# A hybrid attention decoder block on one core: compressed softmax without its table of valid blocks, and the gelu's reciprocals in quarters

## The chip, the cores and the metric

The kernel runs on one core of a Trainium2 chip. The metric is the device time of one execution in microseconds, as the median of several runs. Five engines of the core matter here and are named as the profile names them: PE (TensorE, matrix products and transposes; PEld is its weight load), DVE (VectorE), ACT (ScalarE), POOL (GpSimd) and SP, whose queue issues the DMAs.

## What is computed

Two layers, each a mixer and a gated feed-forward block, over 512 positions of width 1024. The mixer has three groups of heads beside each other: four "forgetting" heads (f), eight heads of native sparse attention (n) in three branches, and four dilated heads (d). The change touches the compressed branch of the n heads. There, keys and values are averaged into 31 blocks by a small network with a gelu, each query attends to the blocks that end at or before it, and the result is weighted by a gate:

```python
k_cmp = nsa_compress(kc, ...)            # gelu(win @ w1) @ w2
s_c = einsum('bqgrd,bngd->bgrqn', qb, k_cmp) * ATTN_SCALE
p_c = masked_softmax(s_c, cmp_end[None, :] <= qpos[:, None])
#   s = where(mask, scores, -1e30);  e = where(mask, exp(s - max), 0)
#   p = e / max(sum(e), 1e-30)
o_c = einsum('bgrqn,bngd->bqgrd', p_c, v_cmp)
o = gate_c * o_c + gate_s * o_s + gate_w * o_w       # gate = sigmoid(...)
```

The first 31 queries have no valid block, and their o_c is zero.

## The kernel before

All matrix products are made in three passes (high part by high part, high by low, low by high), and PE is the engine that most of the program is laid out around. Per layer there is the mixer's stage (here from about 60 to 310 us, and again from 737 to 987 us), in which a loop over units (lines 1240 to 1253) runs. A **unit** is one head, one branch and one of four tiles of 128 queries (t = 0 to 3). A **slot** is one pass of that loop. In a slot i the stages of several units are issued: the scores of unit i (`st_scores`), the maximum of unit i-1 on DVE (`st_max`, line 1126) and its exponential on ACT (`st_exp`, line 1131), the normalisation of unit i-2 (`st_norm`: a small reciprocal on DVE, line 1139, and a multiplication on POOL, line 1143), the transposes of unit i-4 on PE (`st_turn`, line 1156), their evacuation one slot later (lines 1167 and 1172), and the product with the values at i-7. Tiles t = 0 and t = 1 share one bank of scores, one reciprocal and one set of transposes. Unit 0 of layer 0 has its scores at 62 us; unit 33, the one named most below, has t = 1.

Between the stages a slot gives room to other work. First a **step** (`step`, line 1062) takes the next piece of the projections (`proj256`: dv, dq, dk and so on, four row tiles by two halves of the depth, in two PSUM banks), with a budget of 0.8 steps to a slot, so that every fifth slot (36, 41, 46, 51, 56) has none. Then `chain_step` (line 1069) moves the generator `cmp_pieces` (line 938) on by one `yield`: one piece of the compressed branch to a slot. At the slot's end, when the compressed probabilities are complete (`store["pc"]`) and a pair of heads has its sum, `cmp_values` (line 1212) issues the compressed branch's product with the values for one pair.

`cmp_pieces` goes through: the polynomial of the gelu on POOL (941 to 943), the split of w2 and the exponential (946 to 948), one addition and two reciprocals of half the columns each (950 to 952), the multiplication on POOL (954), an empty slot, two transposes (959), their evacuation (965 to 970), an empty slot, then 18 products into two PSUM tiles `pk` and `pv` (973 to 985), their evacuation to `kcm` and `vcm` (991 to 997). From there ten slots run a small softmax for the four query tiles, in which a tile's scores, exponential, normalisation, transposes and evacuation are issued at lags of 0, 1, 3, 5 and 6 slots (`c_scores`, `c_exp`, `c_norm`, `c_turn`, `c_keep`). In this trace the products `pk` and `pv` are issued in slot 40, the four `c_scores` in slots 42 to 45, the four `c_turn` in slots 47 to 50, and `cmp_values` for the first pair in slot 51, for the second in slot 55.

PSUM has eight banks in four tags: three of "acc", one of "o", two of "s", two of "pt". Projections hold two of "acc" at a time, and `cmp_pieces` takes its tiles from the same tag (CT = "acc"). `st_turn`, the transposes of the projections (line 737) and `cmp_values` take "pt". Rows of the softmax, rotated projections and the temporaries of `cmp_pieces` share ten SBUF buffers of the tag "r" (NROW).

Within this loop PE's order is the order of the program (`manual_schedule` for PE). The orders of DVE, ACT and POOL are not: a planner of the framework, with its own idea of durations, puts each instruction into its engine's queue, and the engine then takes them strictly in that order.

Of the kernel before, what the change touches and what calls it, by code (L numbers as in the profile page):

```python
# [9 lines left out]
F32 = mybir.dt.float32  # L10
# [3 lines left out]
ALU = mybir.AluOpType  # L14
# [10 lines left out]
NST = 4  # L25
# [49 lines left out]
def tile_hybrid_block(  # L75
# [6 lines left out]
    nc = tc.nc  # L82
    PS = bass.MemoryType.PSUM
    const = ctx.enter_context(tc.tile_pool(name="const", bufs=1))
# [10 lines left out]
    def nm(p):  # L95
        uid[0] += 1
        return f"{p}_{uid[0]}"
# [7 lines left out]
    def rt(shape=(128, 512), dt=F32):  # L105
        return rowp.tile(list(shape), dt, tag="r", name=nm("r"))

    def st(n, tag="sm"):
        return small.tile([128, n], F32, tag=tag, name=nm("sm"))
# [7 lines left out]
    def bc(ap, axis, n):  # L117
        a = ap.unsqueeze(axis)
        shape = list(a.shape)
        shape[axis] = n  # L120
        return a.to_broadcast(shape)
# [326 lines left out]
    for l in range(DEPTH):  # L448
# [129 lines left out]
        gates = small.tile([128, NST, 24], F32, tag="gates", bufs=1, name=nm("gates"))  # L578
# [35 lines left out]
        if l == 0:  # L614

            dint = rt(dt=I32)
            nc.gpsimd.iota(dint, pattern=[[-1, 512]], base=384, channel_multiplier=1)
            dflt = rt()
            nc.vector.tensor_copy(dflt, dint)
            cmask = const.tile([128, 512], F32, name="cmask")  # L620
            nc.vector.tensor_scalar(cmask, dflt, 0.0, BIG, op0=ALU.is_lt, op1=ALU.mult)
            dmask = const.tile([128, 512], F32, name="dmask")
            cnt = rt()
            nc.vector.tensor_scalar(cnt, dflt, 128.0, None, op0=ALU.is_le)
            for m in (3, 15):
                mi = rt(dt=I32)
                nc.vector.tensor_scalar(mi, dint, m, None, op0=ALU.bitwise_and)
                mf = rt()
                nc.vector.tensor_copy(mf, mi)
                nc.vector.scalar_tensor_tensor(cnt, mf, 0.0, cnt, op0=ALU.is_equal, op1=ALU.add)  # L630
            ge0 = rt()
            nc.vector.tensor_scalar(ge0, dflt, 0.0, None, op0=ALU.is_ge)
            nc.vector.tensor_mul(cnt, cnt, ge0)
            nc.vector.tensor_scalar(dmask, cnt, 0.0, BIG, op0=ALU.is_equal, op1=ALU.mult)
            for v, lg in ((2.0, -math.log(2.0)), (3.0, -math.log(3.0))):
                t = rt()
                nc.vector.tensor_scalar(t, cnt, v, lg, op0=ALU.is_equal, op1=ALU.mult)
                nc.vector.tensor_add(dmask, dmask, t)

            ci = rt((128, NST, 32))  # L640
            nc.gpsimd.iota(ci, pattern=[[128, NST], [-16, 32]], base=-31, channel_multiplier=1,
                           allow_small_or_imprecise_dtypes=True)
            cvalid = const.tile([128, NST, 32], F32, name="cvalid")
            nc.vector.tensor_scalar(cvalid, ci, 0.0, None, op0=ALU.is_ge)
            cinv = const.tile([128, NST, 32], F32, name="cinv")
            nc.vector.tensor_scalar(cinv, ci, 0.0, BIG, op0=ALU.is_lt, op1=ALU.mult)

            odd = const.tile([128, 2], F32, name="odd")
            oi = small.tile([128, 1], I32, tag="oi", bufs=1, name="oi")
            nc.gpsimd.iota(oi, pattern=[[0, 1]], base=0, channel_multiplier=1)  # L650
            nc.vector.tensor_scalar(oi, oi, 32, None, op0=ALU.bitwise_and)
            nc.vector.tensor_copy(odd[:, 1:2], oi)
            nc.vector.tensor_scalar(odd[:, 0:1], odd[:, 1:2], 0.0, None, op0=ALU.is_equal)
            nc.vector.tensor_scalar(odd[:, 1:2], odd[:, 1:2], 0.0, None, op0=ALU.is_gt)
            vcm = const.tile([128, 2, 2, 2, 64], F32R, name="vcm")

        nc.vector.tensor_scalar(gates, gates, 1.0, None, op0=ALU.add)
        nc.vector.reciprocal(gates, gates)

        mix, sums = {}, {}  # L660
        OFIRST = (0, 1, 2, 3)
# [88 lines left out]
        def main_pieces():  # L750
# [54 lines left out]
            def hidden(kv):  # L805
                while len(wins.get(kv, ())) < 2:
                    yield
                ph = ps("acc")
                for c in range(4):
                    hi, lo = getw(l, "w1", kv, c, pre=PRE)  # L810
                    for i in range(4):
                        j = 4 * c + i
                        w = wins[kv][j // 8][:, j % 8].rearrange("p u n -> p (u n)")
                        mm(ph[:, 0:256], w, hi[:, i, :], j == 0, False)
                        mm(ph[:, 0:256], w, lo[:, i, :], False, j == 15)
                    yield
                tmp = rt((128, 256))
                rows = slice(64 * kv, 64 * kv + 64)
                nc.scalar.activation(tmp[rows, :], ph[64:128, 0:256], AF.Copy)
                nc.vector.tensor_add(xc[rows, :], ph[0:64, 0:256], tmp[rows, :])  # L820
                if kv == 1:
                    chain.append(cmp_pieces(xc, w2r))
# [115 lines left out]
        def cmp_pieces(xc, w2r):  # L938

            t1, t2 = rt((128, 256)), rt((128, 256))  # L940
# [7 lines left out]
            nc.scalar.activation(t2, t1, AF.Exp, scale=-2.0 * math.sqrt(2.0 / math.pi))  # L948
            yield
            nc.vector.tensor_scalar(t2, t2, 1.0, None, op0=ALU.add)  # L950
            for c in range(2):
                nc.vector.reciprocal(t2[:, 128 * c:128 * c + 128], t2[:, 128 * c:128 * c + 128])
            yield
            nc.gpsimd.tensor_mul(xc, xc, t2)
            yield
            yield
# [38 lines left out]
            for u in range(2):  # L995
                nc.scalar.activation(vcm[:, :, 0, u, :], src, AF.Copy, scale=odd[:, u:u + 1])
                nc.vector.scalar_tensor_tensor(vcm[:, :, 1, u, :], src, odd[:, u:u + 1], f(vcm[:, :, 0, u, :]),
                                               op0=ALU.mult, op1=ALU.subtract)
# [26 lines left out]
            def c_norm(t):  # L1025
                row = rows[t]
                dn = st(8, "cm")
                nc.gpsimd.tensor_mul(row, row, bc(cvalid[:, t], 1, 8))
                nc.vector.tensor_reduce(dn, row, axis=AX.X, op=ALU.add)
                nc.vector.tensor_scalar(dn, dn, 1e-30, None, op0=ALU.max)  # L1030
                nc.vector.reciprocal(dn, dn)
                nc.vector.tensor_mul(dn, dn, gates[:, t, 0:24:3])
                nc.gpsimd.tensor_mul(row, row, bc(dn, 2, 32))
# [17 lines left out]
            for i in range(NST + CL[3]):  # L1051
                for lag, fn in zip(reversed(CL), (c_keep, c_turn, c_norm, c_exp)):
                    if 0 <= i - lag < NST:
                        fn(i - lag)
                if i < NST:
                    c_scores(i)
                yield
# [365 lines left out]
```

## Time and profile before

| | us |
|---|---|
| median of 3 runs | 1368.08 (1367.97 to 1368.92) |
| profiled execution, its own time | 1369.85 |
| its span, first to last instruction | 1367.9 |
| PE busy | 1338.0 |
| DVE busy | 850.4 |
| ACT busy | 728.2 |
| POOL busy | 287.0 |

The span is what the profiler saw between the first and the last instruction; the profiled execution's own time has 1.95 us around it. An engine is busy while one of its instructions runs; an idle time in brackets behind a row is the time that its engine stood still before it, with the instruction that is taken to have ended the wait. The name is inferred: of several awaited things it is the one that came last by the profile.

### The profile page before, as it was taken

What the parts mean: (1) busy time and instruction counts of PE and PEld (TensorE: products, weight loads), DVE (VectorE), ACT (ScalarE), POOL (GpSimd) and SP (SyncE); (2) the same over time, 40 slices, a digit from 0 to 9 for tenths busy, and PEclk for the clock granted to TensorE, in tenths of its full rate; (3) what the DMA queues carried; (4) which work ended last, traced back from release to release, by engine and by line L of the source; (5) the groups of instructions that cost most, each with busy time, mean ns of one, the idle gap of its engine ahead of it and who ended that gap; (6) DMA issues with size and microseconds to landing.
All of it is one profiled execution on the core that took longest, in us unless ns stands there. A gap on an engine that the chain in (4) does not pass through costs nothing.

```text
span 1367.9 us, 21028 instructions
## 1 busy us (share of the span) xinstructions
PE 1338.0 (98%) x7855; PEld 1177.9 (86%) x7855; DVE 850.4 (62%) x1893; ACT 728.2 (53%) x1506; POOL 287.0 (21%) x343
## 2 busy tenths in 40 slices
PE   9999999999999999999999999999999999999997
PEld 8899998978888888888898999999798888888886
DVE  7677787677755555433464887777876555554334
ACT  6567767777533333333465677667774333333232
POOL 2364753341000000000004647634210000000000
PEclk9999999999999999999999999999999999999999
DMA  6323311131333333333333242111323333332231
GB/s 181 94 63 115 104 35 48 58 128 33 107 93 103 97 92 96 104 93 123 111 96 93 63 139 63 47 41 58 120 62 98 103 92 93 104 97 92 94 122 62
DMA packets 145517, 123.74 MB, mean 90 GB/s; under 512 B 8264, under 2 KB 135688, under 8 KB 145416
## 3 DMA queue, kind: packets, MB, share of 16 engines
q1 hardware_dynamic: 145416, 122.40, 29.5%
q8 instruction: 62, 1.02, 0.3%
q14 instruction: 39, 0.32, 0.1%
HBM read 118.19 MB, written 4.19 MB: 89 GB/s over the span
## 4 chain that ended last, share of the span: by engine, by line
PE 85%; DVE 7%; ACT 4%; POOL 2%; issue 2%; DMA 0%; SPq 0%; ACTq 0%; POOLq 0%; DVEq 0%
PE acc L115 39%; PE s L115 19%; PE pt L115 13%; PE o L115 10%; PE pt L1156 3%; POOL wt L795 1%; PE pt L737 1%; DVE hl L271 1%; DVE pl L1172 1%; DVE r L1126 1%; ACT r L1131 1%; DVE x L913 0%; ACT hh L270 0%; ACT h L310 0%; ACT ph L1167 0%
## 5 line engine op out<-in xcount | busy, mean ns | idle before, releaser
L154 DVE TENSOR_TENSOR wl_up<-raw_up,wh_up 128x1024 fp32r<-128x1024 f32 x78 | 95.6, 1225 | 170.8 <-ACT wh_up L146 170.8
L146 ACT ACTIVATE wh_up<-raw_up 128x1024 fp32r<-128x1024 f32 (+1 forms) x90 | 89.6, 1001 | 160.4 <-PE acc L115 68.1
L154 DVE TENSOR_TENSOR wl_wd<-raw_wd,wh_wd 128x1024 fp32r<-128x1024 f32 x42 | 51.5, 1225 | 133.7 <-ACT wh_wd L146 133.7
L146 ACT ACTIVATE wh_wd<-raw_wd 128x1024 fp32r<-128x1024 f32 x42 | 44.5, 1060 | 144.8 <-PE pt L115 135.5
L1143 POOL TENSOR_SCALAR r<-r,sm,gates 128x128 f32<-128x128 f32 (+3 forms) x128 | 86.4, 683 | 126.1 <-DVE sm L1139 82.3
L1131 ACT ACTIVATE r<-r,sm 128x128 f32<-128x128 f32 x192 | 106.7, 557 | 9.3 <-DVE sm L1126 8.4
L115 PE MATMUL acc<-hh,wl_up 128*128 128x512 f32 (+1 forms) x272 | 102.4, 376 | 0.0
L115 PE MATMUL acc<-hl,wh_up 128*128 128x512 f32 (+1 forms) x272 | 102.4, 376 | 0.0
L115 PE MATMUL acc<-hh,wh_up 128*128 128x512 f32 (+1 forms) x272 | 102.4, 376 | 0.0
L150 POOL TENSOR_TENSOR wl_kc<-raw_kc,wh_kc 128x512 fp32r<-128x512 f32 x8 | 11.8, 1490 | 417.6 <-ACT wh_kc L146 416.8
L115 PE MATMUL s<-k,q 128*128 128x512 f32 (+3 forms) x384 | 96.2, 337 | 0.6 <-DVE sm L1126 0.6
L1172 DVE TENSOR_TENSOR pl<-pt,ph 128x384 fp32r<-128x384 f32 x144 | 85.6, 596 | 17.3 <-ACT ph L1167 15.9
L1167 ACT ACTIVATE ph<-pt 128x384 fp32r<-128x384 f32 x144 | 75.4, 523 | 29.1 <-PE pt L1156 27.9
L1126 DVE CUSTOM_DVE_ANT_0 r<-s,cmask 128x128 f32<-128x128 f32 (+3 forms) x160 | 76.0, 482 | 20.6 <-PE s L115 16.2
L1156 PE MATMUL pt<-ident,r 128*128 128x128 f32 x480 | 77.5, 276 | 7.0 <-DVE pl L1172 5.5
L115 PE MATMUL acc<-wh_wd,gh 128*128 128x512 f32 x252 | 83.7, 389 | 0.0
L115 PE MATMUL s<-hh,wh_up 128*128 128x512 f32 (+1 forms) x224 | 80.4, 359 | 0.0
L115 PE MATMUL s<-hl,wh_up 128*128 128x512 f32 (+1 forms) x224 | 80.4, 359 | 0.0
L115 PE MATMUL s<-hh,wl_up 128*128 128x512 f32 (+1 forms) x224 | 80.4, 359 | 0.0
L1347 ACT ACTIVATE r<-r 128x512 f32<-128x512 f32 x44 | 27.8, 632 | 85.7 <-DVE r L1328 85.5
L1156 PEld LDWEIGHTS pt<-ident,r 128*128 128x128 f32 x480 | 55.4, 141 | 15.9 <-POOL r L1143 6.8
L115 PE MATMUL acc<-wh_wo,mix 128*128 128x256 f32 (+1 forms) x296 | 67.6, 305 | 0.0
(439 smaller groups left out, 4121.2 us busy)
## 6 DMA issues: line engine op xcount, KB each, us to landing
raw_up<-in_w_up_dram SPq DMA_DIRECT2D x88, 512.0 KB, 3.8
raw_wd<-in_w_down_dram SPq DMA_DIRECT2D x44, 512.0 KB, 3.4
raw_wo<-in_w_out_dram SPq DMA_DIRECT2D x16, 512.0 KB, 3.5
x<-in_x_dram SPq DMA_DIRECT2D x8, 512.0 KB, 5.9
raw_nq<-in_w_in_dram SPq DMA_DIRECT2D x8, 512.0 KB, 3.7
raw_w<-in_cmp_w_k_dram SPq DMA_DIRECT2D x8, 512.0 KB, 4.0
raw_w<-in_cmp_w_v_dram SPq DMA_DIRECT2D x8, 512.0 KB, 4.2
raw_fk<-in_w_in_dram SPq DMA_DIRECT2D x4, 512.0 KB, 5.9
```

What stands on the lines that cost most here:

```text
L115: nc.tensor.matmul(o, lhsT=lhsT, rhs=rhs, start=start, stop=stop, skip_group_check=True)
L146: nc.scalar.activation(hi[:, ks], raw[:, ks], AF.Copy)
L154: nc.vector.tensor_sub(lo[:, ks], raw[:, ks], f(hi)[:, ks])
L271: nc.vector.scalar_tensor_tensor(lo, src, gain[:, k:k + 1], f(hi), op0=ALU.mult, op1=ALU.subtract)
L737: nc.tensor.transpose(p[:, 128 * s:128 * s + 128], tl[s][:, 128 * j:128 * j + 128], ident)
L1126: nc.vector.tensor_tensor_reduce(row[:, 0:n], u["S"][:, 0:n], u["mask"][:, 512 - n:512], op0=ALU.add, op1=ALU.min, scale=1.0, scalar=3.0e3 ...
L1131: nc.scalar.activation(row[:, 0:n], row[:, 0:n], AF.Exp, scale=-1.0, bias=sm_[0], accum_out=sm_[1])
L1143: nc.gpsimd.tensor_scalar(row[:, 0:n], row[:, 0:n], z["sm"][2], g_, op0=ALU.mult, op1=ALU.mult)
L1156: nc.tensor.transpose(p[:, 128 * c:128 * c + 128], blocks[z], ident)
L1167: nc.scalar.activation(hi, src, AF.Copy)
L1172: nc.vector.tensor_sub(*u["lo"])
L1347: nc.scalar.activation(cd[0], cd[0], AF.Silu)
```

## The change

1. The table `cvalid` (128 by 4 by 32, which blocks are valid) goes. In its place stands `cany`, one number for each of the first 128 queries: whether its first block is valid.
2. After the gates are computed, the compressed gates of query tile 0 are multiplied by `cany`, once in a layer, on DVE. A query without a valid block has the same score everywhere (the 1e30 of `cinv`), so that its exponentials are all one; its gate is now zero.
3. In `c_norm`, the multiplication by `cvalid` on POOL and the maximum with 1e-30 on DVE go, in each of the four tiles of a layer.
4. In `cmp_pieces`, the two reciprocals of 128 columns in one slot become four of 64 columns, each followed by a `yield`. What follows in `cmp_pieces` is issued three slots later.

```diff
-            cvalid = const.tile([128, NST, 32], F32, name="cvalid")
-            nc.vector.tensor_scalar(cvalid, ci, 0.0, None, op0=ALU.is_ge)
+
+            cany = const.tile([128, 1], F32, name="cany")
+            nc.vector.tensor_scalar(cany, ci[:, 0, 0:1], 0.0, None, op0=ALU.is_ge)
...
         nc.vector.reciprocal(gates, gates)
+
+        nc.vector.tensor_scalar(gates[:, 0, 0:24:3], gates[:, 0, 0:24:3], cany, None, op0=ALU.mult)
...
             nc.vector.tensor_scalar(t2, t2, 1.0, None, op0=ALU.add)
-            for c in range(2):
-                nc.vector.reciprocal(t2[:, 128 * c:128 * c + 128], t2[:, 128 * c:128 * c + 128])
-            yield
+            for c in range(4):
+                nc.vector.reciprocal(t2[:, 64 * c:64 * c + 64], t2[:, 64 * c:64 * c + 64])
+                yield
             nc.gpsimd.tensor_mul(xc, xc, t2)
...
                 dn = st(8, "cm")
-                nc.gpsimd.tensor_mul(row, row, bc(cvalid[:, t], 1, 8))
                 nc.vector.tensor_reduce(dn, row, axis=AX.X, op=ALU.add)
-                nc.vector.tensor_scalar(dn, dn, 1e-30, None, op0=ALU.max)
                 nc.vector.reciprocal(dn, dn)
```

## Rows read from the trace of the kernel before

**Rows 1.** The page, part 1 (engine, busy us, share, instructions) and granted clock.
```profile
PE 1338.0 (98%) x7855; PEld 1177.9 (86%) x7855; DVE 850.4 (62%) x1893; ACT 728.2 (53%) x1506; POOL 287.0 (21%) x343
PEclk9999999999999999999999999999999999999999
```
**Rows 2.** The chain that ended last: start us, length us, what.
```profile
162.38 1.68 DVE r L952 x2
```
**Rows 3.** Timeline of PE: start, length, instruction, [idle before, and who ended it].
```profile
161.70 0.50 PE L115 MATMUL s<-k,q 128*128 128x512 f32 x1 [0.31 <-DVE sm L1126]
166.27 0.52 PE L1156 MATMUL pt<-ident,r 128*128 128x128 f32 x3 [1.52 <-DVE pl L1172]
...
197.80 0.41 PE L1039 MATMUL acc<-ident,r 128*128 128x128 f32 x2 [0.66 <-DVE pcl L1047]
...
219.61 0.52 PE L1156 MATMUL pt<-ident,r 128*128 128x128 f32 x3 [0.52 <-DVE mx L1221]
...
840.89 0.52 PE L1156 MATMUL pt<-ident,r 128*128 128x128 f32 x3 [1.52 <-DVE pl L1172]
```
**Rows 4.** Timeline of DVE and POOL before the stop at 166.27.
```profile
161.21 0.42 DVE L1126 CUSTOM_DVE_ANT_0 r<-s,cmask 128x256 f32<-128x256 f32 x1 [0.33 <-PE pt L737]
162.29 1.76 DVE L952 RECIPROCAL r<-r 128x128 f32<-128x128 f32 x2
163.97 0.11 DVE L1139 RECIPROCAL sm<-sm 128x2 f32<-128x2 f32 x1
...
164.20 0.74 POOL L954 TENSOR_TENSOR r<-r,r 128x256 f32<-128x256 f32 x1 [2.47 <-DVE sm L1139]
164.91 1.00 POOL L1143 TENSOR_SCALAR r<-r,sm,gates 128x128 f32<-128x128 f32 x2
```
**Rows 5.** DVE by line and form, reciprocals: count, busy us, mean ns, idle before.
```profile
L1139 DVE RECIPROCAL sm<-sm 128x1 f32<-128x1 f32 x96 | 15.0, 156 | 10.2 <-ACT r L1131 9.9
L952 DVE RECIPROCAL r<-r 128x128 f32<-128x128 f32 x4 | 3.5, 921 | 0.0
L658 DVE RECIPROCAL gates<-gates 128x96 f32<-128x96 f32 x2 | 1.5, 742 | 0.0
```
**Rows 6.** What `c_norm` loses, by line and form, and a stretch beside POOL.
```profile
L1028 POOL TENSOR_TENSOR r<-r,cvalid 128x256 f32<-128x256 f32 x8 | 5.9, 735 | 2.1 <-ACT r L1022 2.1
L1030 DVE TENSOR_SCALAR sm<-sm 128x8 f32<-128x8 f32 x8 | 2.9, 361 | 0.1
...
191.20 1.29 POOL L150 TENSOR_TENSOR wl_dk<-raw_dk,wh_dk 128x512 fp32r<-128x512 f32 x1
191.54 0.98 DVE L1032 TENSOR_TENSOR sm<-sm,gates 128x8 f32<-128x8 f32 x1
```
**Rows 7.** Timeline: the products into pk and pv, their evacuation, and later scores.
```profile
175.62 1.82 PE L115 MATMUL acc<-r,r 128*64 128x64 f32 x18
177.08 0.45 DVE L993 TENSOR_TENSOR kcm<-acc,kcm 64x64 fp32r<-64x64 f32 x2 [0.42 <-ACT kcm L991]
...
185.31 0.42 PE L115 MATMUL s<-k,q 128*128 128x128 f32 x2
```
**Rows 8.** Timeline: the first `c_turn` and its evacuation on ACT and DVE.
```profile
195.10 0.38 PE L1039 MATMUL acc<-ident,r 128*128 128x128 f32 x2
195.52 0.39 ACT L1046 ACTIVATE pch<-acc 128x256 fp32r<-128x256 f32 x1 [0.70 <-PE acc L1039]
197.26 0.40 DVE L1047 TENSOR_TENSOR pcl<-acc,pch 128x256 fp32r<-128x256 f32 x1
```
**Rows 9.** Timeline: slot 51, the first `cmp_values`, and the start of slot 52.
```profile
203.78 0.48 PE L115 MATMUL s<-k,q 128*128 128x512 f32 x1
204.86 0.49 PE L115 MATMUL pt<-pch,vcm 64*128 64x512 f32 x1
206.12 0.44 PE L115 MATMUL s<-k,q 128*128 128x128 f32 x2
206.22 0.69 DVE L1221 TENSOR_TENSOR mx<-mx,pt 128x512 f32<-128x512 f32 x1 [0.21 <-PE pt L115]
```

## The prediction

> **What bounds the kernel now.** [...] The change adds and removes no work of PE, so it can act only through the 30 us in which PE stands still. The chain that ended last passes, in the stretch of the change, through the pair of reciprocals on line 952 [rows 2]. I then went through PE's timeline for every bracket [rows 3]. From the gelu's start to the transposes behind the second `cmp_values` there are six, and the same six in layer 1; four of them stand in the rows, and one of layer 1. Two carry the case: 1.52 us at 166.27, with its twin at 840.89, and 0.66 us at 197.80.
>
> The long one needs care, for the name in its bracket (line 1172) is not its cause. The transposes need the rows of unit 33, multiplied by POOL. DVE runs both reciprocals of line 952 from 162.29 to 164.05, and the small reciprocal of unit 33 stands right behind them, at 163.97. POOL stands still for 2.47 us, does the gelu's multiplication for 0.74 us and only then the rows, from 164.91 to 165.91 [rows 4]. Everything between 162.4 and 166.2 hangs on the pair.
>
> **The reciprocals in quarters.** A reciprocal takes 156 ns for one column, 742 for 96 and 921 for 128 [rows 5]. By the line from 1 to 96 columns, 64 take 0.156 + 63 x (0.742 - 0.156) / 95 = 0.545 us, four 2.18 us, against 1.84 for the pair: 0.34 us more on DVE in a layer. With one quarter ahead of it, the small reciprocal of unit 33 can run some 1.2 us earlier (1.76 - 0.55), and POOL's 0.74 us is no longer ahead of the rows, because that multiplication is now three slots away. Together that is 1.9 us, more than the 1.52 us of the stop: the stop goes, 2 x 1.52 = 3.04 us in two layers. What is late next is PE itself. I cost the added 0.34 us at nothing, since it is spread over four slots; were DVE's queue full in all of them it would be 0.34 a layer. The 0.31 us at 161.70 stays: there DVE's maximum waited for a row buffer that the transposes of line 737 held [rows 3, 4], ahead of any reciprocal.
>
> [...]
>
> **Three slots later.** Everything behind the reciprocals moves: `pk` and `pv` from slot 40 to 43, `c_scores` to slots 45 to 48, `c_turn` from 47 to 50 to slots 50 to 53, the first `cmp_values` from slot 51 to 54. The second stays in 55, because it waits for its heads, and so the output projection, which waits for that, starts no later. PE's amount of work is unchanged, but it meets other neighbours at three places.
>
> First, `pk` and `pv`. Now they come at the end of dv, when one of its two banks is free. In slot 43 they come after the second step of dq; dq holds one bank, `pk` and `pv` take the others, and dq's third step, in slot 44, needs a bank for its second half. `pk` is given back when DVE has made `kcm`: 175.62 to 177.53, 1.91 us, plus some 0.14 for the signal (taken from 197.66 to 197.80). Until that step PE has the 18 products, 1.82, and scores for 0.42 us [rows 3, 7, 8]. With queues as free as now it is covered by 0.2 us; if ACT and DVE are each in the middle of something (0.7 us each, as line 1221's 0.69 [rows 9]), PE stops for 1.2 us. Bounds 0 to 1.2; I take 0.4, nearer to the row.
>
> Second, `c_turn`. Chain work has a single bank while dq holds two, so each turn waits for the evacuation of the one before. From a turn's start that takes at least 1.35 us (ACT from 0.42 to 0.81, DVE 0.40, signal 0.14) and took 2.70 at 195.10, where DVE came late [rows 8]; PE had 2.04 us of other work and stopped for the 0.66. The second turn now falls into slot 51, which has no step: from the scores at 203.78 to what follows them at 204.86 are 1.08 us, with the 0.14 from turn to scores 1.2 us [rows 9]. It stops for 0.15 to 1.5 us. The third has 2.04 us and stops for 0 to 0.66. Against today's 0.66: between -0.51 and +1.5; I take +0.25, a little below the middle, because DVE has less to do there (next part).
>
> Third, `cmp_values` in slot 54 is followed by the transposes of slots 55 and 57, line 737 twice, and the second `cmp_values`, all through two "pt" banks; this place already has the 0.52 us at 219.61 [rows 3]. One such product takes 206.12 - 204.86 = 1.26 us of PE, and its bank is free 0.69 + 0.14 us after 206.22, 2.19 us from its start; behind it PE has 1.26 and about 0.5 us of scores [rows 9]. Shortfall 0.4, up to 1.1 if DVE is busy, less up to 0.5 where today's stops vanish because PE comes later. Bounds -0.1 to +1.1; I take +0.2.
>
> **The table.** Four multiplications of 735 ns on POOL and four maxima of 361 ns on DVE go in each layer [rows 6]. No PE bracket names them, so I cost them at nothing beyond the allowance above; the cover is PE's own work in slots 45 to 51, and a POOL that is busy for 21% of the span [rows 1]. The table itself was one instruction at the start of layer 0. Added are one comparison of one column, and one multiplication of eight columns in a layer (0.15 to 0.36 us by lines 1139 and 1030 [rows 5, 6]), in DVE's queue before the slots, where the first user of a compressed gate is 100 us away.
>
> **The sum.** A layer: -1.52 + 0.4 + 0.25 + 0.2 = -0.67; two layers -1.34 us. The profiled execution would go from 1369.85 to 1368.5; it lies 1.77 us above the median, and on the median's scale this is 1368.08 - 1.34, about 1366.7. With all bounds low: -1.52 - 0.51 - 0.1 = -2.13, or 1363.8. With all high: -1.52 + 0.34 + 1.2 + 1.5 + 1.1 = +2.62, or 1373.3.
>
> **The rivals.** *Clean move.* The three places cost nothing and the stop at 197.80 goes as well. What speaks for it: DVE's L1032 on eight columns took 0.98 us while POOL ran from 191.20 to 192.49, and L1030 averages 361 ns against 156 for a smaller relative [rows 5, 6]. If POOL's operations hold DVE up, then 4 x 0.735 us less of them frees the evacuations that the turns wait for. Time: -1.52 - 0.4 a layer, 1364.2. [...]
>
> *Quarters that stay together.* The change doesn't do what it says: the four become ready at once, and the planner may queue them back to back, so that the small reciprocal still stands behind all of them. The stop stays, the 0.34 us adds to it, and so does the move: +0.34 + 0.85 a layer, 1370.5. Against it: the program asks for the later quarters after the row work of their slots.
>
> *A bank short, slower.* The third "acc" bank becomes the limit: `pk` and `pv` cost 1.2 and the turns 1.5 more, with pt's 0.2 a loss of 2.9 against 1.52: +1.4 a layer, 1370.9. It decides from 2.9 us of new stops in a layer on (1.52 + 2.74 / 2).
>
> **How the numbers follow.** About 0.2%, 2.7 us, is what a measurement of this kernel can tell from no change: faster means under 1365.3, slower over 1370.8. Forecast 0.50; clean move 0.27; quarters together 0.11; a bank short 0.12. Of the forecast's share 0.03 falls below 1365.3 and 0.02 above 1370.8; the quarters lie just inside, with 0.03 of them outside. Faster 0.30, same 0.53, slower 0.17. The range takes in the clean move and the quarters, 1363.8 to 1370.9.
>
> **What would show it.** In the changed kernel's trace: reciprocals of 64 columns of about 0.55 us, with the maxima and small reciprocals of other units between them; no bracket over 0.5 us at the transposes of unit 33; a bracket at dq's third step or at `pv`; the largest turn bracket in slot 51; one at the transposes behind the first `cmp_values`, near 215 us. The prediction is wrong if the quarters run back to back, if the new brackets in a layer sum to more than 2.9 us, or if the time moves while PE's brackets don't.

## The result and the profile after

The changed kernel takes 1383.66 us at the median of five runs (1378.78 to 1384.19), the kernel before 1368.07 on the same chip (1367.87 to 1368.92): a ratio of 1.0099, with a 95% interval from 1.0087 to 1.0111. It is slower by 15.6 us, far outside the range that was forecast.

The page's first lines of the changed kernel (engine, busy us, share of the span, instructions), which answer to [rows 1]:

```profile
span 1381.7 us, 21034 instructions
PE 1345.2 (97%) x7855; PEld 1183.3 (86%) x7855; DVE 849.6 (61%) x1891; ACT 728.0 (53%) x1506; POOL 280.5 (20%) x335
```

The span has grown by 13.8 us. PE has the same 7855 instructions, so they can lie in two places only: PE stood still for 6.6 us more (36.5 us against 29.9), and it needed 7.2 us more for the same work.

The idle time first. PE's timeline of layer 0, instructions with idle time before them (start, length, instruction, [idle, who ended it]), which answers to [rows 3], and the two long ones of layer 1:

```profile
161.88 0.73 PE L115 MATMUL s<-k,q 128*128 128x512 f32 x2 [0.31 <-DVE sm L1127]
165.77 0.52 PE L1157 MATMUL pt<-ident,r 128*128 128x128 f32 x3 [0.83 <-DVE q L490]
191.27 1.26 PE L115 MATMUL acc<-kcm,q 128*128 128x64 f32 x8 [1.48 <-DVE r L1021]
200.88 1.05 PE L115 MATMUL acc<-kcm,q 128*128 128x64 f32 x8 [2.01 <-DVE acc L473]
213.29 0.41 PE L1040 MATMUL acc<-ident,r 128*128 128x128 f32 x2 [0.90 <-DVE r L476]
221.46 0.63 PE L1157 MATMUL pt<-ident,r 128*128 128x128 f32 x4 [0.21 <-DVE mx L1222]
223.95 0.66 PE L740 MATMUL pt<-ident,r 128*128 128x128 f32 x4 [0.43 <-DVE pl L1173]
225.04 0.50 PE L115 MATMUL pt<-pch,vcm 64*128 64x512 f32 x1 [0.43 <-DVE q L490]
227.21 0.52 PE L1157 MATMUL pt<-ident,r 128*128 128x128 f32 x3 [0.55 <-DVE mx L1222]
...
873.60 1.05 PE L115 MATMUL acc<-kcm,q 128*128 128x64 f32 x8 [1.48 <-DVE r L1021]
883.20 1.05 PE L115 MATMUL acc<-kcm,q 128*128 128x64 f32 x8 [2.01 <-DVE acc L473]
```

The stop at unit 33's transposes fell from 1.52 to 0.83 us, and two stops of 1.48 and 2.01 us stand where there was none: at the second and the fourth `c_scores` (`acc<-kcm,q`). In layer 0 the brackets of this stretch sum to 7.15 us, against 3.65 before, and in layer 1 the difference is the same, 3.5; other places gave back 0.4.

Then the busy time. The granted clock behind the first of these stops, in stretches of 1 us of the changed kernel (stretch, us, busy share and count of PE, PEld, DVE, ACT, POOL, then the granted clock, DMA share, GB/s):

```profile
191.00:192.00 1.00, 0.73 (x7) 0.76 (x7) 0.98 (x4) 0.19 (x2) 0.01 (x1) 0.98 0.13 12
192.00:193.00 1.00, 1.00 (x5) 0.90 (x5) 0.42 (x1) 0.36 (x1) 1.00 (x2) 0.50 0.88 257
193.00:194.00 1.00, 1.00 (x6) 0.80 (x5) 0.31 (x1) 0.06 (x1) 0.26 (x1) 0.50 0.73 255
194.00:195.00 1.00, 1.00 (x6) 1.00 (x5) 0.72 (x3) 0.57 (x2) 0.00 (x0) 0.50 0.00 0
195.00:196.00 1.00, 1.00 (x9) 1.00 (x8) 0.94 (x3) 0.73 (x3) 0.00 (x0) 0.81 0.00 0
196.00:197.00 1.00, 1.00 (x12) 1.00 (x10) 0.81 (x5) 0.19 (x1) 0.84 (x2) 1.00 0.00 0
```

PE is full and does half as many instructions: its granted clock was 0.50 from 192.0 to 195.4, and 1.00 again in the last row. The shares missing to full clock sum to 0.02 + 3 x 0.50 + 0.19 = 1.71 us. The same happens behind the other long stops, four times in the profiled execution (from 192.0, 202.2, 874.6 and 884.9 us), 6.8 us in all up to 1360 us; the end of the program is left out here. The profiled execution of the kernel before has one such fall, here in a stretch of 10 us:

```profile
890.00:900.00 10.00, 8.83 (x52) 7.72 (x51) 6.46 (x15) 5.80 (x14) 3.05 (x4) 0.83 0.15 55
```

It is 1.7 us as well, about the 1.78 us by which that execution lies over its median. In [rows 1] it can't be seen: a digit there stands for 34 us, and 9 for 90% or more. So of the 7.2 us, 6.8 - 1.7 = 5.1 are the clock; some 2.1 us of PE's busy time I could not place. Idle 6.6, clock 5.1 and these 2.1 are the 13.8 us.

### The profile page after: what moved, and what is told of

It reads as the page before. It is cut to its first block, busy times and chain, and to the rows that moved or that the text cites. A ratio compares the mean times of both kernels' runs of the same rounds, so it can differ in the third digit from the quotient of the medians.

```text
span 1381.7 us, 21034 instructions
## 1 busy us (share of the span) xinstructions
PE 1345.2 (97%) x7855; PEld 1183.3 (86%) x7855; DVE 849.6 (61%) x1891; ACT 728.0 (53%) x1506; POOL 280.5 (20%) x335
## 3 DMA queue, kind: packets, MB, share of 16 engines
q8 instruction: 62, 1.02, 0.3%
## 4 chain that ended last, share of the span: by engine, by line
PE 85%; DVE 7%; ACT 5%; issue 2%; POOL 2%; ACTq 0%; DVEq 0%; POOLq 0%
PE acc L115 39%; PE s L115 18%; PE pt L115 13%; PE o L115 10%; PE pt L1157 3%; DVE hl L271 1%; PE pt L740 1%; POOL wt L798 1%; DVE pl L1173 1%; ACT hh L270 1%; ACT r L1132 0%; DVE r L1127 0%; DVE x L916 0%; ACT r L1206 0%; ACT ph L1168 0%
## 5 line engine op out<-in xcount | busy, mean ns | idle before, releaser
L150 POOL TENSOR_TENSOR wl_kc<-raw_kc,wh_kc 128x512 fp32r<-128x512 f32 x8 | 11.6, 1469 | 417.5 <-ACT wh_kc L146 416.7
```

## What makes a `c_scores` wait

The changed kernel's chain of waits through the two stops (start us, length us, what) reads like an explanation:

```profile
188.21 1.25 PE o L115 x8
189.46 0.02 issue
189.49 0.60 ACT r L1206
190.09 0.02 issue
190.11 0.68 DVE mx L1207
190.79 0.34 DVE r L1021
191.13 0.14 issue
191.27 1.26 PE acc L115 x8
```

And the timeline of DVE before the second of them:

```profile
198.91 0.23 DVE L471 TENSOR_TENSOR rope<-acc,ss 128x64 f32<-128x64 f32 x1 [2.06 <-PE acc L115]
...
199.65 0.41 DVE L1020 TENSOR_TENSOR r<-acc,cinv 128x256 f32<-128x256 f32 x1
200.33 0.41 DVE L1021 TENSOR_TENSOR r<-r,acc 128x256 f32<-128x256 f32 x1
```

While dq holds two "acc" banks, one is left, and a tile's scores can start only when DVE has read the tile before out of it, with the two additions of `c_exp` (lines 1020 and 1021). These are issued one slot after the scores. In slot 46, where a head of the attention ends, its result is issued ahead of them: PE's product with the values, ACT's copy (1206), DVE's addition (1207). DVE took its queue in order: line 1021 started at 190.79, behind 1207, though line 1020 had been done since 188.24; 1207 started at 190.11, behind ACT's copy, and the copy at 189.49, behind PE's own product, which ended at 189.46. PE had little left to do, as slot 46 has no step. In slot 48 the first rotation of dq (471) stands ahead of the additions. PE had finished the third tile's scores at 197.14, but DVE stands still for 2.06 us for the rotation's input, which PE completes at 198.87. PE goes on at 200.88, 0.14 us after the end of line 1021 at 200.74 (at the first stop 0.15 us after its end at 191.12); line 473, the name in the bracket, ends at 200.88 itself, too late to have released anything. Before the change, the four `c_scores` were issued in slots 42 to 45 and met neither.

This is the **queue theory**: the loss is where the additions stand in DVE's queue. A rival, the **bank theory**, says that a single free bank is too little in these slots wherever the additions stand. A third is that the quarters or the missing table cost the time by themselves, and the move nothing.

## Experiments: which part costs the time

**The table alone**: the change without item 4.

> The table of valid blocks goes, the gelu keeps its two reciprocals in one slot, so nothing behind them moves. Theory of the place (what costs is that the compressed branch's scores now meet slots 46 and 48): no stop at c_scores, the 1.52 us at the transposes of unit 33 stays, the time is that of before less at most 2 x 0.66 us of the c_turn stop: 1366.7 to 1368.5 us. Rival, theory of the table (POOL and DVE reordered by the missing operations): stops of 1.5 and 2.0 us at c_scores, 1376 us or more.

1368.59 us, a ratio of 1.0005 (0.9996 to 1.0015): no difference. PE's stop of 0.66 us at the second `c_turn` [rows 3] is gone, no `c_scores` waits, and the stop at the transposes of unit 33 stays at 1.51. The 1.3 us of the two `c_turn` stops don't show in the time; the profiled execution, 1370.91 us, has two falls of the clock where the one of before has one.

**The quarters alone**: item 4 in the kernel before, with its table.

> The quarters one to a slot, with the table kept. Theory of the place: the two stops at c_scores of about 1.5 and 2.0 us a layer with the lower clock behind each, as in the changed kernel: 1379 to 1386 us. Theory of the table: 1365 to 1368 us.

1382.95 us, 1.0109 (1.0094 to 1.0124): the whole loss. PE's timeline of this kernel, layer 0:

```profile
190.83 1.05 PE L115 MATMUL acc<-kcm,q 128*128 128x64 f32 x8 [1.47 <-DVE r L1018]
198.78 1.05 PE L115 MATMUL acc<-kcm,q 128*128 128x64 f32 x8 [1.94 <-DVE acc L473]
```

**The move alone**: the kernel before with three empty slots behind its pair of reciprocals.

```diff
             yield
+            yield
+            yield
+            yield
             nc.gpsimd.tensor_mul(xc, xc, t2)
```

> The kernel before with three empty slots behind its pair of reciprocals: nothing is split and nothing removed, the compressed branch only comes three slots later. Theory of the place: the 1.52 us at unit 33's transposes stays and the two stops at c_scores come: 1380 to 1388 us, the slowest of these four. Rival, theory of the split (reciprocals of 64 columns, spread over DVE's queue, delay the softmax's own work): 1367 to 1371 us.

1382.69 us, 1.0106 (1.0091 to 1.0121), with stops of 1.47 us at 191.64 and 1.94 at 201.13. Nothing is computed otherwise and nothing is added: three empty slots cost what the change costs.

**The quarters in one slot**: the changed kernel with one `yield` behind all four.

> The changed kernel with its four quarters in one slot, so that nothing behind them moves. Theory of the place: no stop at c_scores; the stop at unit 33's transposes is between 0 and 1.5 us, as DVE's queue mixes the quarters with other work or not: 1364 to 1368.5 us. Theory of the split: 1372 us or more.

1369.81 us, 1.0006 (0.9996 to 1.0015), a little over the band that was expected. No `c_scores` waits. The quarters run back to back, and unit 33's transposes stop PE for 1.54 us: as the rival of quarters that stay together says of that stop, the gain is gone.

The quarters' arithmetic and the table are cleared; the move carries the loss.

**One and two empty slots** in place of three.

> The kernel before with one empty slot behind its pair: the scores of the compressed branch come in slots 43 to 46. Theory of DVE's queue: the fourth c_scores falls into slot 46, where its predecessor's adds stand behind the end of a head, and stops PE for about 1.5 us; none in slot 48. With one fall of the clock a layer, about half of the loss of three slots: 1372 to 1377 us. Theory of the bank: no stop, since dq's first half is still running beside it: 1367 to 1369 us.

> The kernel before with two empty slots behind its pair: scores in slots 44 to 47. Theory of DVE's queue: the third c_scores, in slot 46, stops PE for about 1.5 us, the fourth, in slot 47, does not (dq's first rotation is queued in slot 48): 1372 to 1377 us. A loss in proportion to the shift would be two thirds of three slots', 1377 to 1379 us.

One slot: 1375.13 us, 1.0051 (1.0036 to 1.0067). Two: 1373.88, 1.0041 (1.0027 to 1.0055). The first row is of the kernel with one empty slot, the second of the one with two; in each layer each has this one long stop at a `c_scores`:

```profile
193.21 1.05 PE L115 MATMUL acc<-kcm,q 128*128 128x64 f32 x8 [1.47 <-DVE r L1019]
```
```profile
192.66 1.05 PE L115 MATMUL acc<-kcm,q 128*128 128x64 f32 x8 [1.47 <-DVE r L1020]
```

The price doesn't grow with the slots. With one, two or three slots some tile's scores fall into slot 46, and there is the stop of 1.47; only with three does the last tile reach slot 48, and there is the second. The loss goes by what stands in a slot.

## Experiment: queue or bank

In the changed kernel `c_exp` of a tile, which begins with the two additions, is issued right behind its scores, in the same slot. PE's order and the number of free banks stay.

```diff
-                for lag, fn in zip(reversed(CL), (c_keep, c_turn, c_norm, c_exp)):
+                for lag, fn in zip(reversed(CL), (c_keep, c_turn, c_norm)):
...
                     c_scores(i)
+                    c_exp(i)
```

> The changed kernel, with the adds that read a tile's compressed scores issued in the slot of the scores itself instead of the next one. PE's order and every slot of its work stay; only DVE's, POOL's and ACT's queues change, so that the adds stand ahead of the head's end of slot 46 and of dq's first rotation in slot 48. Theory of DVE's queue (PE stops because the adds stand behind instructions that wait for PE themselves): both stops and both falls of the clock go, 1365 to 1369.5 us. Rival, theory of the bank (one bank for four score tiles, in slots with little other work of PE, whatever DVE's order): stops of 1 us or more stay at c_scores, 1375 us or more.

1370.99 us, 1.0017 of before (1.0008 to 1.0026), 12.7 us less than the changed kernel. DVE's timeline of this kernel in slot 46, and the one `c_scores` that still waits:

```profile
187.53 0.42 DVE L1020 TENSOR_TENSOR r<-acc,cinv 128x256 f32<-128x256 f32 x1 [1.10 <-PE acc L115]
...
188.21 0.42 DVE L1021 TENSOR_TENSOR r<-r,acc 128x256 f32<-128x256 f32 x1
...
189.88 0.68 DVE L1208 TENSOR_TENSOR mx<-o,r 64x512 f32<-64x512 f32 x1 [0.73 <-ACT r L1207]
...
193.38 1.05 PE L115 MATMUL acc<-kcm,q 128*128 128x64 f32 x8 [0.65 <-DVE r L1021]
```

The additions now run ahead of the head's end (1208), and the stops of 1.48 and 2.01 us are gone. What is left is 0.65 us at the third tile, where an evacuation that waits for ACT stands ahead of them. The clock doesn't fall once before 1360 us. The brackets explain 2 x (1.48 + 2.01 - 0.65) = 5.7 us and the four falls 6.8, together 12.5 of the 12.7. The queue theory stands. The bank theory falls as a cause of its own: the single bank is the condition, but with the additions in time it costs 0.65 us. The time is about 1.5 us over the band that was expected; 2 x 0.65 = 1.3 of it is the stop that is left, which was not foreseen.

## Experiments: the stop of 1.52 us, and better places

**No reciprocals**: the kernel before without line 952, so that the gelu's division is left out.

> The kernel before without the gelu's reciprocals: the division of the gelu is left out, so its values are other ones; every slot stays. It prices the reciprocals by their whole absence, 1.84 us of DVE a layer. If POOL's rows alone were late, the stop at unit 33's transposes goes to nothing: 1364.5 to 1365.5 us. If the bank of the transposes, which DVE gives back behind its other evacuations, is late next, a stop of 0.2 to 0.8 us stays: 1365.5 to 1367 us.

1366.71 us, 0.9982 (0.9973 to 0.9991). The transposes of unit 33 follow without any idle time:

```profile
165.37 0.52 PE L1154 MATMUL pt<-ident,r 128*128 128x128 f32 x3
```

So the whole stop hangs on the pair of reciprocals, and this is what the gain was worth at most: 3.0 us by brackets. Of these, 1.6 reach the median, so that the time lies in the band that was expected for a stop that stays; the profiled execution has a fall of the clock from 11 to 15 us, far ahead of the first edited line. This run doesn't tell whether the rows or a "pt" bank ended the stop, as both come earlier in it.

**Halves, one to a slot, nothing moved**: the change with two reciprocals of 128 columns in two slots, and one of the two `yield`s behind the multiplication taken out, so that the gelu's transposes come in their old slot.

```diff
             for c in range(2):
                 nc.vector.reciprocal(t2[:, 128 * c:128 * c + 128], t2[:, 128 * c:128 * c + 128])
-            yield
+                yield
             nc.gpsimd.tensor_mul(xc, xc, t2)
             yield
-            yield
```

> The table goes, and the reciprocals stay halves, one to a slot; the empty slot behind the gelu's multiplication is taken out, so that the transposes and everything behind them keep the slots that they had. Theory of the place: no stop at c_scores, the stop at unit 33's transposes falls from 1.5 to 0.8 us or less, as in the changed kernel: 1364.5 to 1368 us. Rival: one half in the queue is enough to keep the stop (1.5 us): 1368 to 1370 us.

1367.33 us, 0.9991 (0.9982 to 1.0000). The stop at unit 33 falls to 1.07 us, not to the 0.8 that was expected, and the stop at the second `c_turn` to 0.15. The name in the bracket is now POOL's multiplication of the gelu, but that ends at 165.76, when PE goes on; line 490 on DVE ended 0.15 us before. That kernel with the second `cmp_values` two slots later:

```diff
-                whole.append((u["h"] // 2, slot[0] + 1))
+                whole.append((u["h"] // 2, slot[0] + (3 if u["h"] // 2 == 1 else 1)))
```

> The version with halves one to a slot and nothing moved, and the second compressed product with the values two slots later, in slot 57 in place of 55. If the three brackets near 216 to 220 us (0.47, 0.17, 0.52) come from five users of two pt banks in slots 54 to 57, the last two shrink to 0.3 us or less together, and the fall of the clock that follows them in some layers goes: 1363.5 to 1366.5 us. If the brackets only move by two slots: 1366.5 to 1368 us.

1366.38 us, 0.9986 (0.9977 to 0.9995): faster than both kernels, by 2.0 us against the kernel before. The time is in the first band that was expected, but not for its reason: the stops of 0.17 and 0.52 us around that product have not shrunk, they have become one of 0.66. What is gone in the profiled execution is the fall of the clock that the halves have in theirs, from 218.9 us.

**Quarters with nothing moved**: four quarters in three slots, the last two of them with the multiplication, and one `yield` behind it taken out, so that the gelu's transposes come in their old slot.

> The changed kernel with its quarters in three slots (one, one, and two with the multiplication), and the empty slot behind the multiplication taken out, so that the transposes and all behind them keep their slots. Theory of the place: no stop at c_scores; at unit 33's transposes 0.8 us as in the changed kernel, against 1.1 with halves: 1366 to 1368 us. If the split in quarters is worth its whole stop, as the prediction had it: 1364 to 1365.5 us.

1369.55 us, 1.0007 (0.9999 to 1.0016). PE's timeline of this kernel:

```profile
165.51 0.52 PE L1157 MATMUL pt<-ident,r 128*128 128x128 f32 x3 [0.83 <-DVE q L490]
168.89 0.44 PE L962 MATMUL acc<-ident,r 128*128 128x128 f32 x2 [1.43 <-POOL r L958]
```

The time is over the band that was expected. The stop at unit 33 falls as in the changed kernel, and 1.43 us come back at the gelu's own transposes, which now wait for the multiplication. The quarters need their three slots; without them the stop only moves.

## Why the prediction was wrong, point by point

**The step that failed** is "Three slots later". It lists the move of `c_scores` to slots 45 to 48 and then prices three places, `pk` and `pv`, `c_turn` and `cmp_values`. `c_scores` is not among them, so its term was nothing; it measured 3.49 us in a layer, more than all the others together. For `c_turn` the text says that chain work has a single bank while dq holds two, so that each turn waits for the evacuation of the one before. The same sentence holds for `c_scores`, one stage earlier. With the slots worked out, slot 46 could have been looked up as slot 51 was: no step there, and a head's end in DVE's queue.

**The second error: the clock.** The sum takes PE at full clock throughout [rows 1], and the stops of 1.52 us in the kernel before were indeed followed by no fall. Each long `c_scores` stop was followed by one in the profiled execution, 1.71 us more, nearly doubling its price.

**The stop at unit 33.** That the pair of reciprocals is behind it was right: without them the stop is gone. The path was wrong. The text set aside the name in the bracket of before, line 1172 [rows 3], and took the rows of unit 33 for the last wait. DVE's row of that line in the kernel before:

```profile
165.44 0.69 DVE L1172 TENSOR_TENSOR pl<-pt,ph 128x512 fp32r<-128x512 f32 x1
```

It ends at 166.13, 0.14 us before PE goes on at 166.27; the rows were ready on POOL at 165.91 [rows 4]. The transposes need a "pt" bank as well as the rows, and the bank came last: its evacuation stood in DVE's queue behind the pair, line 490 and a maximum. So the text priced the wait that ended last but one, and named PE itself as late next where it was the bank: 0.83 us of the stop stayed. DVE's timeline of the changed kernel:

```profile
162.48 0.55 DVE L955 RECIPROCAL r<-r 128x64 f32<-128x64 f32 x1
162.94 0.10 DVE L1140 RECIPROCAL sm<-sm 128x2 f32<-128x2 f32 x1
163.08 0.68 DVE L490 SCALAR_TENSOR_TENSOR q<-pt,q 64x512 fp32r<-64x512 f32 x1
163.80 0.55 DVE L955 RECIPROCAL r<-r 128x64 f32<-128x64 f32 x1
164.27 0.63 DVE L1127 CUSTOM_DVE_ANT_0 r<-s,cmask 128x512 f32<-128x512 f32 x1
...
164.93 0.69 DVE L490 SCALAR_TENSOR_TENSOR q<-pt,q 64x512 fp32r<-64x512 f32 x1
```

The quarters are apart, and the small reciprocal comes after the first of them: 0.46 us from the first reciprocal's start (162.94 - 162.48), where it was 1.68 before (163.97 - 162.29 [rows 4]). That is 1.22 us earlier, as forecast. The rows of unit 33 were ready on POOL at 164.15, 1.6 us before PE went on. But a "pt" bank came back only at 165.62, when line 490 was done, which stood in DVE's queue behind the second quarter and a maximum, and PE went on 0.15 us later.

**Sizes.** A quarter took 541 ns, forecast 545:

```profile
L955 DVE RECIPROCAL r<-r 128x64 f32<-128x64 f32 x8 | 4.3, 541 | 0.1
```

| place, us in a layer | forecast | measured |
|---|---|---|
| unit 33's transposes | -1.52 | -0.69 |
| `pk`, `pv` and dq's third step | +0.4 | 0 |
| `c_scores` | not priced | +3.49 |
| `c_turn` | +0.25 | +0.24 |
| `cmp_values` and its "pt" neighbours | +0.2 | +0.46 |
| sum of the brackets | -0.67 | +3.50 |
| clock | 0 | two falls of 1.71 |

For `c_turn` the size is right by luck. The second turn, in slot 51, has no stop, where 0.15 to 1.5 us were forecast, and the third stops for 0.90 us (at 213.29), over its bound of 0.66. The second turn and DVE's part of the first one's evacuation, in the changed kernel:

```profile
209.86 0.38 PE L1040 MATMUL acc<-ident,r 128*128 128x128 f32 x2
210.16 0.42 DVE L1048 TENSOR_TENSOR pcl<-acc,pch 128x256 fp32r<-128x256 f32 x1
```

The turn starts before that evacuation does, so here it did not wait for the bank of the one before. For `cmp_values` the four brackets from 221.46 to 227.21 sum to 1.62 us against 1.16 before, within its bounds of -0.1 to +1.1. At `pk` and `pv` no bracket stands anywhere, as the row of 1.91 us had said.

**The rivals.** *Clean move.* This rival takes POOL to hold DVE up. With the table alone the second turn's stop does go, and the multiplication with the gates (L1032 [rows 6]) falls from at most 977 ns to at most 211. No run isolates POOL as the cause of either: the operation beside the 977 ns was the split of a weight (L150 [rows 6]), which stays and only runs at another moment. The time stayed (1.0005). *Quarters that stay together*: they did not. With all four in one slot they did, and 1369.81 us is near the 1370.5 forecast, but by luck: that sum holds 0.85 us a layer for the move, which this kernel doesn't make. Without it, it gives 1368.8. *A bank short* has the sign and the resource, the third "acc" bank, but its two terms are those that measured 0 and +0.24; it was right on neither place nor size.

**Of the conditions named for being wrong** one held: the new brackets were to sum to more than 2.9 us in a layer, and they are 3.49 + 0.24 + 0.46 = 4.2.

## What to carry to other kernels

When a chain moves by a few slots, go through every stage of it that needs a scarce buffer, and for each new slot read what stands ahead of its release in the releasing engine's queue; DVE's queue, taken in order here, passed on the wait of what stood first, PE's wait for its own product, and PE stopped for 1.48 us. An empty slot in a hand-made order is not free: three of them cost 1% here. Where the release can be issued earlier, in the slot of the work itself, most of the price goes: 12.7 of the 15.6 us here.

## What the runs showed of the hardware

DVE took its queue in order. The third tile's scores were done at 197.14 and DVE stood still until 198.91, yet line 1020 ran at 199.65, behind the rotation that was issued first.

A stop of PE can cost more than its length. Of the 16 `c_scores` stops of 1.47 to 2.01 us in the profiled executions of five kernels (the changed one, the quarters alone, and one, two and three empty slots), 10 were followed by a fall of the granted clock to 0.50, each with about 1.7 us of full clock missing; the stops of 1.51 to 1.54 us at unit 33's transposes were followed by none. In the kernel before, the clock goes on at full behind that stop:

```profile
166.00:167.00 1.00, 0.73 (x7) 0.76 (x8) 0.95 (x3) 0.97 (x4) 1.00 (x1) 1.00 0.04 8
167.00:168.00 1.00, 1.00 (x11) 1.00 (x10) 0.97 (x7) 0.87 (x4) 1.00 (x2) 1.00 0.00 0
168.00:169.00 1.00, 1.00 (x8) 0.96 (x8) 0.41 (x2) 0.45 (x2) 1.00 (x2) 1.00 0.00 0
```

With three empty slots it was the first of the two stops in layer 0 and the second in layer 1. Nor does a fall need a long stop. The fall of the kernel before starts at 894.0 us, at a stop of a third of the length, behind the second `cmp_values`:

```profile
894.20 0.87 PE L1156 MATMUL pt<-ident,r 128*128 128x128 f32 x3 [0.53 <-DVE mx L1221]
```

Six more falls stand within 0.7 us of the end of this stop: two each with the table alone and with the quarters in one slot, one each with the quarters alone and with the halves. So the length doesn't decide alone, and what does stays open.

A fall may also not be lost in full. Where the second `c_scores` stop is not followed by one (three empty slots in layer 0, the quarters alone in layer 1), PE stops for 1.02 and 1.03 us at a unit's scores some 9 us later; where it is, in four layers, it doesn't. Why was not tested. The falls also spread the times of one program: the changed kernel ran in 1378.78 us with a mean clock of 0.998 and in 1384.19 with 0.994.
